# A decoder trunk on one core: the residual kept transposed, product-key scores left unscaled, sums of squares taken by matmul

## The chip, the cores and the metric

The kernel runs on one core of one Trainium2 chip. The metric is device microseconds of the whole launch; the median of three runs is compared. The traces show five engines. PE does matmuls and transposes (its weight loads are listed apart as PEld), DVE is the vector engine, ACT the scalar engine, POOL is GpSimd, and SP only issues DMAs. ACT and POOL can issue DMAs as well.

## The reference

The input x has 256 tokens (S) of 1024 features (D). Two residual layers follow, each with a mixer and a product-key expert layer ("PEER").

```python
h = x
for layer in (0, 1):
    xn = rmsnorm(h, norm_mix[layer])
    h = h + (attn_retention_mixer if layer == 0 else short_conv_mixer)(xn)
    h = h + peer(rmsnorm(h, norm_ffn[layer]))
return rmsnorm(h, final_norm)

def rmsnorm(x, g):
    return x * lax.rsqrt(mean(x * x, -1) + EPS) * g
def peer(t):                      # 8 heads, 128 x 128 experts, top 16
    q = (t @ w_q).reshape(n_tok, 8, 2, 128)
    sc = einsum('thpd,hpnd->thpn', q, sub_keys)
    s1, i1 = top_k(sc[:, :, 0], 16);  s2, i2 = top_k(sc[:, :, 1], 16)
    top_s, pos = top_k(all sums s1 + s2, 16);  eidx = the pair's expert number
    gate = softmax(top_s)
    return sum_k gate * gelu(t . u[eidx]) * v[eidx]
```

## The kernel before

**Stages.** In the profiled execution: the input projection of the even mixer to 103 us, its output projection to 128.6 us, the PEER queries of layer 0 to 183 us, the U pass over all experts to about 492 us, the V pass to 747 us, then the odd mixer, its output projection from 820.7 us, the queries from 844 us, U and V again, and the last norm from 1453 us. All four engines run orders that are written out by hand in program order, so each engine works strictly through its own list.

**Weights.** `Stream` loads weight tiles of 128 x 1024 into a ring of eight slots (SP issues, L153). Most tiles are split: ACT makes `hi` (L176), then DVE or POOL makes `lo` = raw - hi in bf16 (L178). A product takes three matmuls: hi with the high part of the activation, hi with its low part, and lo with its bf16 copy `Xb`. `u_tile` (L292) makes a 128 x 256 transposed output so. `u_pair` (L308) makes two at once, and goes through the eight feature blocks k in order, so that it can start when the first blocks of the activation `x2` are there; it calls `norm.tail(k)` between them.

**Residual.** `h` holds two halves of 128 tokens by 1024 features. The projections want activations with features on partitions. So `Norm.turn` (L435) transposes h on PE, and `Norm.parts` (L447) makes `x2[:, k, 0]` on ACT (L454), `x2[:, k, 1]` on DVE (L455) and, per two blocks, `Xb` on POOL (L458). `v_phase` (L336) makes the output projection of a mixer with tokens on partitions: for each of eight weight tiles four groups of three matmuls of 512 columns (L331 to L333), then DVE adds each quarter to h (L356). `square` (L395) sums squares on ACT.

**PEER.** Per query tile f (16 of them): a `u_tile`, four passes for scores (L1160), an ACT copy that multiplies by the norm's reciprocal root (L1163), DVE's top-16 search (L1147 to L1155) paced by a `Pump`. `Norm.rows` (L522) prepares in steps f = 2 to 5 the rows `XG` that the gathered experts meet (L535, L539, L541) and the scaled `xf` for the dense pass (L528, L532). The first 96 tokens use gathered expert rows (`Gather`, L992): 192 indirect DMAs of 128 x 1024 per layer (L1029), each eaten by one DVE instruction (L1039 for U, L1050 for V). The other 160 tokens go densely through all 128 expert tiles: L1417 in the U pass, L1520, L1560 and L1562 in the V pass, where `weight_rest` (L1435, DVE) and `weight_parts` (L1428, ACT) split the tiles.

**End of V.** The output of V is built transposed in eight PSUM banks `vo[b]`. In steps 16 to 23 PE adds h into them, by matmuls with the identity (L1550, L1551). The last three weight tiles go block by block; behind each block `fold(b)` makes `XT` (ACT L1573, DVE L1574). In layer 0 `Folded` makes `x2` from XT (L576, L577, L580), transposes XT back into h during the pair (`back`, L548; ACT L593, L609). In layer 1 `Final` squares and scales XT (L641 to L644), sums squares by matmul with a column of ones (L660), transposes (L653), and writes out.

**Start.** x comes in natural layout by one DMA on SP and one on ACT; 24 dummy matmuls (`busy`, L379) run meanwhile; `Norm.first` (L494) turns it.

Of the kernel before, what the change touches and what calls it, by code (L numbers as in the profile page):

```python
# [225 lines left out]
def trunk_kernel(ctx, tc, x, small, cst, mcst, ew_in, ew_out, ow_in, ow_out, wq, keys, pu, pe_, pv, pvn, pun, gains, out):  # L226
# [28 lines left out]
    srcs += [(ow_in[f], i > 1 and i % 2 == 1) for i, f in enumerate(OF)]  # L255
# [3 lines left out]
    h = pers.tile([P, 2, D], F32, tag="h", name="h")  # L259
# [76 lines left out]
    def v_phase(n, part, each, norm):  # L336


        accs = [acc_tile(i, nm("acc")) for i in range(4)]
        for i in range(n - 2):  # L340
            each(i)
            w = st.next()
            p = part(i)
            for a in range(4):
                run(v_mm(w, p, accs[a], a // 2, a % 2, i == 0, False))
        each(n - 2)
        each(n - 1)
        ws = [st.next(), st.next(ahead=False)]
        st.ahead(0)
        ps = [part(n - 2), part(n - 1)]  # L350
        for a in range(4):
            for j in range(2):
                run(v_mm(ws[j], ps[j], accs[a], a // 2, a % 2, False, j == 1))
                if a == 3 and j == 0:
                    norm.amid()
            v.tensor_tensor(h[:, a // 2, (a % 2) * 512:(a % 2 + 1) * 512], accs[a],  # L356
                            h[:, a // 2, (a % 2) * 512:(a % 2 + 1) * 512], OP.add)
            norm.done(a, accs[a])
# [25 lines left out]
    class Sums:  # L384
# [10 lines left out]
        def square(self, a, junk):  # L395
            th, ch = a // 2, a % 2
            act.activation(junk, h[:, th, ch * 512:(ch + 1) * 512], AF.Square, accum_out=self.w[:, th, ch:ch + 1])
# [21 lines left out]

    class Norm(Sums):  # L420
# [3 lines left out]
        def __init__(self, gi):  # L424
            super().__init__()
            self.gi = gi
            self.ps = {}

        def warm(self):

            if self.gi in (1, 3):
                nc.sync.dma_start(XG[:, 1, :], gains[self.gi // 2])
            self.table()

        def turn(self, a):  # L435


            th, ch = a // 2, a % 2
            if th == 0:
                for j in range(2):  # L440
                    self.ps[ch, j] = acc_tile(j, nm("xt")) if ch else side_tile(nm("xt"))
            for k in range(4):
                kk = ch * 4 + k
                o = (k // 2 * 2 + th) * P
                pe.transpose(self.ps[ch, k % 2][:, o:o + P], h[:, th, kk * P:(kk + 1) * P], ident)

        def parts(self, ch, ks=range(4)):  # L447

            x2 = xv["x2"]
            for k in ks:  # L450
                kk = ch * 4 + k
                ps = self.ps[ch, k % 2][:, k // 2 * S:(k // 2 + 1) * S]
                gain = G[:, (3 + self.gi) * ND + kk:(3 + self.gi) * ND + kk + 1]
                act.activation(x2[:, kk, 0, :], ps, AF.Copy, scale=gain)  # L454
                v.scalar_tensor_tensor(x2[:, kk, 1, :], ps, gain, x2[:, kk, 0, :].bitcast(F32),  # L455
                                       op0=OP.mult, op1=OP.subtract)
                if k % 2:
                    gp.tensor_copy(Xb[:, kk - 1:kk + 1, :], x2[:, kk - 1:kk + 1, 0, :].bitcast(F32))  # L458

        def done(self, a, junk):  # L460

            if a == 1:
                self.turn(0)
            if a < 3:
                self.square(a, junk)
            if a == 1:
                self.mean0(0)
                self.root(0)
            if a == 2:
                self.turn(1)  # L470
                self.rstd(0)
                self.mean0(1)
                new_x2()
            if a == 3:
                self.parts(0, (2, 3))
                self.junk = junk

        def amid(self):

            self.turn(2)  # L480
            self.parts(0, (0, 1))

        def tail(self, k):

            if k != 1:
                return
            self.turn(3)
            self.parts(1)
            self.square(3, self.junk)
            self.root(1)  # L490
            self.rstd(1)
            st.ahead(0)

        def first(self, junk):  # L494

            new_x2()
            for a in (0, 2, 1, 3):
                self.turn(a)
            self.parts(0, (0, 1))
            st._split()  # L500
            self.parts(0, (2, 3))
            st._split()
            self.parts(1)
            st._split()
            self.junk = junk

        def late(self, th):
# [5 lines left out]
            self.rstd(th)  # L513

# [7 lines left out]
        def rows(self):  # L522

            x2 = xv["x2"]

            def whole():
                XF = new_xf()
                v.tensor_tensor(XF, x2[:, :, 0, TG:].bitcast(F32), x2[:, :, 1, TG:].bitcast(F32), OP.add)  # L528

            def scaled():  # L530
                ps = self.spread()
                v.tensor_tensor(xv["xf"], xv["xf"], ps[:, None, TG:].to_broadcast([P, ND, TD]), OP.mult)  # L532

            def fetched():
                v.scalar_tensor_tensor(XG[:TG, 0, :], h[:TG, 0, :], self.scale(0)[:TG], XG[:TG, 1, :],  # L535
                                       op0=OP.mult, op1=OP.mult)
# [6 lines left out]
            return [fetched, doubled, whole, scaled]  # L543

    def back(fq, XT, th, ch):

        for b in range(4):
            pe.transpose(fq[:, b * P:(b + 1) * P], XT[:, ch * 4 + b, th * P:(th + 1) * P], ident)  # L548

    class Folded(Norm):  # L550


        def begin(self, XT, fold):

            st.parts()
            new_x2()
            self.XT = XT
            self.fq = {}
            self.fold = fold
            st.parts()  # L560

        def block(self, b, pend):

            self.fold(b)
            if b:
                self.ready(b - 1)
            if b == 5:
                st.parts()
            if b == ND - 1:
                self.ready(b)  # L570

        def ready(self, k):

            x2, XT = xv["x2"], self.XT
            gain = G[:, (3 + self.gi) * ND + k:(3 + self.gi) * ND + k + 1]
            act.activation(x2[:, k, 0, :], XT[:, k, :], AF.Copy, scale=gain)  # L576
            v.scalar_tensor_tensor(x2[:, k, 1, :], XT[:, k, :], gain, x2[:, k, 0, :].bitcast(F32),  # L577
                                   op0=OP.mult, op1=OP.subtract)
            if k % 2:
                gp.tensor_copy(Xb[:, k - 1:k + 1, :], x2[:, k - 1:k + 1, 0, :].bitcast(F32))  # L580

        def tail(self, k):

            if k == 1:
                st.parts()
# [1072 lines left out]
```

## Time and profile before

| | |
|---|---|
| median of 3 runs | 1475.15 us (1473.57 to 1475.42) |
| profiled execution, own time | 1473.25 us |
| its span, first to last instruction | 1471.5 us |
| mean granted clock of PE | 0.996 |
| PE busy | 1426.3 us, 97% of the span |
| DVE, ACT, POOL busy | 84%, 55%, 53% |
| moved by DMA | 531.78 MB, mean 361 GB/s |

The own time is 1.75 us above the span (what lies around the first and last instruction). In timeline lines the first number is the start in us, the second the time from the first to the last of the instructions merged into the line; the bracket is idle time of that engine before it and what ended it. In a table of windows the columns are the stretch, its length, busy time (and instructions) of PE, PEld, DVE, ACT and POOL, the granted clock, the mean busy share of the DMA engines, and the rate.

### The profile page before, as it was taken

Reading aid. Unit: us, or ns where it says so; the run is one execution under the profiler, and the core shown is the slowest. Engines: PE = TensorE matmul, PEld = TensorE weight load, DVE = VectorE, ACT = ScalarE, POOL = GpSimd, SP = SyncE. Lnnn points to the kernel's source line nnn. Section 1 sums busy time; section 2 is a strip of 40 time slices with the busy share of each in tenths; the row PEclk is TensorE's granted clock in tenths of the full one; section 3 lists DMA queues with packets and bytes.
Section 4 is the critical chain, followed back from the end, with each engine's and each line's share of the span. In section 5 each row is a group of like instructions: output and inputs, shape, how many; then the busy total and the mean of one; then the engine's idle time right before and its main releaser. Section 6 shows DMA issues by size and latency. Waiting matters only on the chain.

```text
span 1471.5 us, 29881 instructions
## 1 busy us (share of the span) xinstructions
PE 1426.3 (97%) x11246; PEld 1327.1 (90%) x11260; DVE 1238.5 (84%) x2505; ACT 804.0 (55%) x1872; POOL 779.3 (53%) x508
## 2 busy tenths in 40 slices
PE   9999999999999999999999999999999999999997
PEld 5667999999999999988998699999999999998887
DVE  5637999968898689989976589998788869999997
ACT  5555512248786556665563463212887746665654
POOL 6754545555655247655444374465555626665440
PEclk9999999999999999999999999999999999999999
DMA  8546899999999999999975588999999999999994
GB/s 325 191 156 247 315 370 392 400 414 411 409 406 404 400 393 412 415 416 414 411 264 181 180 303 342 403 382 406 409 412 413 410 411 392 408 415 414 415 415 181
DMA packets 113729, 531.78 MB, mean 361 GB/s; under 512 B 13168, under 2 KB 13424, under 8 KB 83888
## 3 DMA queue, kind: packets, MB, share of 16 engines
q1 hardware_dynamic: 57024, 325.06, 55.8%
q0 software_dynamic: 56416, 204.29, 35.1%
q8 instruction: 88, 1.44, 0.4%
q10 hardware_dynamic: 144, 0.52, 0.1%
q14 instruction: 57, 0.47, 0.1%
HBM read 527.93 MB, written 1.05 MB: 359 GB/s over the span
## 4 chain that ended last, share of the span: by engine, by line
PE 37%; DVE 23%; DMA 23%; issue 9%; POOL 6%; ACT 1%; DVEq 0%; SPq 0%; POOLq 0%; ACTq 0%
PE hid L1417 11%; DMA grow<-pvn,ig 9%; DMA rows<-pvn,ig 9%; PE vo L1560 5%; DMA rows<-pun,ig 4%; POOL rows L1029 4%; DVE rows L1039 4%; PE vo L1562 3%; PE hid L299 2%; PE vo L1520 2%; DVE hg L1149 2%; DVE hg L1155 2%; DVE hg L1151 2%; POOL grow L1029 2%; PE ea L331 2%
## 5 line engine op out<-in xcount | busy, mean ns | idle before, releaser
L1417 PE MATMUL hid<-xf,raw 128*128 128x160 f32 x3328 | 477.2, 301 | 7.8 <-DVE hg L1460 7.8
L1417 PEld LDWEIGHTS hid<-xf,raw 128*128 128x128 f32 x3328 | 457.8, 190 | 10.0 <-DVE hg L1460 9.9
L1428 ACT CAST vhi<-raw 128x1024 fp32r<-128x1024 f32 x222 | 229.9, 1047 | 191.7 <-DMA raw<-pv 96.7
L1029 POOL DMA_INDIRECT rows<-pvn,ig x128 | 217.7, 1700 | 183.9 <-DVE gacc L1050 150.1
L1435 DVE TENSOR_TENSOR vlo<-raw,vhi 128x1024 bf16<-128x1024 f32 x222 | 266.5, 1216 | 22.5 <-ACT vhi L1428 22.1
L1029 POOL DMA_INDIRECT rows<-pun,ig x128 | 163.4, 1277 | 116.1 <-DVE rows L1039 59.1
L1560 PE MATMUL vo<-ko,vhi 128*128 128x320 f32 x1200 | 213.6, 320 | 0.0
L178 POOL TENSOR_TENSOR lo<-raw,hi 128x1024 bf16<-128x1024 f32 x70 | 168.0, 2410 | 85.1 <-ACT hi L176 77.2
L1560 PEld LDWEIGHTS vo<-ko,vhi 128*128 128x128 f32 x1200 | 178.0, 189 | 0.0
L1562 PE MATMUL vo<-hb,vlo 128*128 128x160 bf16 x1776 | 162.0, 234 | 15.8 <-DVE vlo L1435 15.6
L1050 DVE SCALAR_TENSOR_TENSOR gacc<-rows,ghid,gacc 128x1024 f32<-128x1024 f32 x124 | 158.3, 1277 | 17.9 <-DMA rows<-pvn,ig 17.6
L1039 DVE SCALAR_TENSOR_TENSOR rows<-rows,xg 128x1024 f32<-128x1024 f32 x128 | 154.9, 1217 | 21.2 <-DMA rows<-pun,ig 20.9
L1029 POOL DMA_INDIRECT grow<-pvn,ig x64 | 117.7, 1838 | 94.7 <-DVE gacc L1050 77.2
L1457 ACT ACTIVATE hg<-hid 128x160 f32<-128x160 f32 (+14 forms) x240 | 61.9, 265 | 192.3 <-PE hid L1417 192.2
L1562 PEld LDWEIGHTS <-vlo 128*128 128x128 bf16 x1776 | 117.9, 98 | 42.4 <-DVE vlo L1435 22.2
L1029 POOL DMA_INDIRECT grow<-pun,ig x64 | 84.2, 1316 | 79.0 <-DVE grow L1039 51.9
L1367 ACT ACTIVATE ko<-ko,idxT 128x128 f16<-128x128 f16 x320 | 101.6, 391 | 38.3 <-DVE ko L1352 38.2
L176 ACT CAST hi<-raw 128x1024 fp32r<-128x1024 f32 x100 | 102.3, 1046 | 29.0 <-issue 17.4
L299 PE MATMUL hid<-x,hi 128*128 128x256 f32 x800 | 107.4, 287 | 3.9 <-DVE z L982 2.0
L299 PEld LDWEIGHTS hid<-x,hi 128*128 128x128 f32 x800 | 98.6, 190 | 5.0 <-issue 3.1
L1560 PE MATMUL vo<-xf,vhi 128*128 128x320 f32 x576 | 102.7, 321 | 0.0
L1370 ACT ACTIVATE ko<-ko,idxT 128x128 f16<-128x128 f16 x320 | 101.2, 389 | 0.0
(258 smaller groups left out, 2238.4 us busy)
## 6 DMA issues: line engine op xcount, KB each, us to landing
raw<-pv SPq DMA_DIRECT2D x128, 1024.0 KB, 9.4
raw<-pu SPq DMA_DIRECT2D x104, 1024.0 KB, 8.2
raw<-wq SPq DMA_DIRECT2D x32, 512.0 KB, 4.0
raw<-ew_in SPq DMA_DIRECT2D x28, 512.0 KB, 4.6
raw<-ow_in SPq DMA_DIRECT2D x24, 512.0 KB, 4.9
hg<-pe_ SPq DMA_DIRECT2D x22, 512.0 KB, 6.4
raw<-ew_out SPq DMA_DIRECT2D x8, 512.0 KB, 4.0
raw<-ow_out SPq DMA_DIRECT2D x8, 512.0 KB, 3.5
```

Source lines behind the costliest of these rows:

```text
L176: self.nc.scalar.copy(hi, t)
L178: eng.tensor_tensor(lo, t, hi.bitcast(F32), OP.subtract)
L299: pe.matmul(ps[:, :S], hi[:, k * P:(k + 1) * P], A2[:, k, s_, :], start=k == 0 and s_ == 0, stop=False)
L1029: gp.indirect_dma_start(self.row(s_), None, table, bass.IndirectOffsetOnAxis(IG[:, 0, s_ % STEPS:s_ % STEPS + 1].bitcast(U32), 0))
L1039: v.scalar_tensor_tensor(r, r, 1.0, XG[:, q % 2, :], op0=OP.mult, op1=OP.mult, accum_out=w)
L1050: v.scalar_tensor_tensor(self.acc[q], r, w, self.acc[q], op0=OP.mult, op1=OP.add)
L1367: act.activation(hi[:, j], lo[:, j], AF.Copy, scale=idxT[:, 1, t:t + 1])
L1417: pe.matmul(ps[:, :TD], w[k], xv["xf"][:, k, :], start=k == 0, stop=k == ND - 1)
L1428: act.copy(whi[j], raw)
L1435: v.tensor_tensor(wlo[j], raw, whi[j].bitcast(F32), OP.subtract)
L1560: pe.matmul(vo[b][:, TG:S + TD], hi[:, b * P:(b + 1) * P], hs, **m)
L1562: pe.matmul(vo[b][:, TG:S], lo[:, b * P:(b + 1) * P], hb, **m)
```

## The change

- `h` becomes 128 features by 8 blocks by 256 tokens. x comes transposed from HBM by two ACT DMAs; a natural copy `xn` goes into XG and serves for the first norm's squares alone. SP issues the weights first. 34 dummy matmuls instead of 24. `late` runs one step later.
- `v_phase` puts out transposed blocks: per weight tile and block two matmuls of 256 columns with hi and one with lo. The last two tiles go block by block. `Norm` replaces `Folded`: behind each block DVE folds into h, ACT makes the high part and a square, DVE the low part of the block before.
- All `turn` and `back` transposes and the identity matmuls of V go. `fold(b)` at the end of V is two DVE additions into h.
- Sums of squares: DVE adds the squares down to 128 x 512 during the pair, and `sums` makes four matmuls with a column of ones behind the third query tile. In the odd mixer a fourth tile is multiplied before the norm's factor is spread.
- Scores are copied unscaled; the exponential of the gates takes the factor.
- `rows` runs in f = 3 to 5: `fetched_rows` transposes 96 tokens of h with eight PE transposes; `dense` scales in eight DVE instructions instead of two.
- The last norm: squares in XG, the scaling of blocks moves from DVE to ACT, one DVE instruction fewer at the end, two of the four output DMAs go by ACT.
- The lo parts of the fourth odd input tile move from POOL to DVE.

```diff
-    h = pers.tile([P, 2, D], F32, tag="h", name="h")
+    h = pers.tile([P, ND, S], F32, tag="h", name="h")
@@ v_phase
+        for i in range(n - 2):
+            ...
+            for b in range(ND):
+                high(b, w, p, i == 0 and b < 4)
+            for b in range(ND):
+                low(b, w, p, False)
+        ws = [st.next(ahead=False) for _ in range(2)]
+        norm.begin(lambda b: v.tensor_tensor(h[:, b, :], out_of(b), h[:, b, :], OP.add))
+        for b in range(ND):
+            for w, p in zip(ws, ps):
+                high(b, w, p, False)
+            for j, (w, p) in enumerate(zip(ws, ps)):
+                low(b, w, p, j == 1)
+            norm.block(b, [])
@@ Norm
+        def begin(self, fold):
+            if self.mixes:
+                st.parts()
+            new_x2()
+            self.fold = fold
+            self.sq = [XG[:, 0, :], new_xf().rearrange("p k t -> p (k t)")[:, :D]]
+            if self.mixes:
+                st.parts()
+        def block(self, b, pend):
+            self.fold(b)
+            self.high(b)
+            act.activation(self.sq[b // 4][:, b % 4 * S:(b % 4 + 1) * S], h[:, b, :], AF.Square)
+            if b:
+                self.low(b - 1)
+            if b == ND - 1:
+                self.low(b)
+        def tail(self, k):
+            if k == 1:
+                st.parts()
+            if k == 2:
+                a, b = self.sq
+                v.tensor_tensor(a, a, b, OP.add)
+                v.tensor_tensor(a[:, :2 * S], a[:, :2 * S], a[:, 2 * S:], OP.add)
+            if k == 7 and self.mixes:
+                st.parts()
+                st.parts()
+        def sums(self):
+            ssq = side_tile(nm("ssq"))
+            for n in range(2):
+                for th in range(2):
+                    o = n * S + th * P
+                    pe.matmul(ssq[:, th:th + 1], self.sq[0][:, o:o + P], C[:, C_ONE:C_ONE + 1], ...)
+            ...
@@ end of V
-                if 16 <= i < 16 + ND:
-                    pe.matmul(vo[b][:, :P], h[:, 0, c], ident, **m)
-                    pe.matmul(vo[b][:, P:S], h[:, 1, c], ident, **m)
             def fold(b):
-                act.copy(XT[:, b, :], vo[b][:, :S])
-                v.tensor_tensor(XT[:, b, TG:], vo[b][:, S:S + TD], XT[:, b, TG:], OP.add)
+                v.tensor_tensor(h[:, b, :], vo[b][:, :S], h[:, b, :], OP.add)
+                v.tensor_tensor(h[:, b, TG:], vo[b][:, S:S + TD], h[:, b, TG:], OP.add)
@@ scores, queries
-                    act.activation(sc(th, f), ps[...], AF.Copy, scale=before.scale(th))
+                    act.copy(sc(th, f), ps[...])
-                if f == 1:
+                if f == 2:
+                    before.sums()
                     rows = before.rows()
-                if 1 < f < 6:
-                    rows[f - 2]()
+                if 2 < f < 6:
+                    rows[f - 3]()
@@ start
+        nc.scalar.dma_start(G, small)
+        for a in range(2):
+            nc.scalar.dma_start(h[:, a * 4:(a + 1) * 4, :], x[:, a * 4:(a + 1) * 4, :])
         ...
+        for th in range(2):
+            nc.scalar.dma_start(XG[:, th, :], xn[th])
+        nc.sync.dma_start(C, cst)
+        busy(34)
```

More of the change, by code (lines that the diff above doesn't have):

```diff
@@ L225, in trunk_kernel @@
 @with_exitstack
-def trunk_kernel(ctx, tc, x, small, cst, mcst, ew_in, ew_out, ow_in, ow_out, wq, keys, pu, pe_, pv, pvn, pun, gains, out):
+def trunk_kernel(ctx, tc, x, xn, small, cst, mcst, ew_in, ew_out, ow_in, ow_out, wq, keys, pu, pe_, pv, pvn, pun, gains, out):
     nc = tc.nc
@@ L339, in v_phase, with out_of, high, low @@
         accs = [acc_tile(i, nm("acc")) for i in range(4)]
+        def out_of(b):
+            return accs[b % 4][:, b // 4 * S:(b // 4 + 1) * S]
+        def high(b, w, p, first):
+            c = slice(b * P, (b + 1) * P)
+            m = dict(stop=False, skip_group_check=True)
+            pe.matmul(out_of(b), w[0][:, c], p[0], start=first, **m)
+            pe.matmul(out_of(b), w[0][:, c], p[1], start=False, **m)
+        def low(b, w, p, last):
+            pe.matmul(out_of(b), w[1][:, b * P:(b + 1) * P], p[2], start=False, stop=last, skip_group_check=True)
         for i in range(n - 2):
@@ L426, in __init__ @@
             self.gi = gi
-            self.ps = {}
+            self.mixes = gi % 2 == 0
         def warm(self):
-            if self.gi in (1, 3):
+            if not self.mixes:
                 nc.sync.dma_start(XG[:, 1, :], gains[self.gi // 2])
             self.table()
[L435 to L445, printed above, removed]
@@ L460, in done @@
[L460 to L481, printed above, removed]
@@ L483, in tail, with gain, high, low @@
[L483 to L492, printed above, removed]
+        def gain(self, k):
+            return G[:, (3 + self.gi) * ND + k:(3 + self.gi) * ND + k + 1]
+        def high(self, k):
+            act.activation(xv["x2"][:, k, 0, :], h[:, k, :], AF.Copy, scale=self.gain(k))
+        def low(self, k):
+            x2 = xv["x2"]
+            v.scalar_tensor_tensor(x2[:, k, 1, :], h[:, k, :], self.gain(k), x2[:, k, 0, :].bitcast(F32),
+                                   op0=OP.mult, op1=OP.subtract)
+            if k % 2:
+                gp.tensor_copy(Xb[:, k - 1:k + 1, :], x2[:, k - 1:k + 1, 0, :].bitcast(F32))
@@ L494, in first @@
         def first(self, junk):
             new_x2()
[L497 to L504, printed above, removed]
-            self.junk = junk
+            self.junk = junk
+            for k in range(0, ND, 2):
+                for j in (k, k + 1):
+                    self.high(j)
+                for j in (k, k + 1):
+                    self.low(j)
+                if k < 6:
+                    st._split()
@@ L957, in odd_mixer @@
                     third = u_tile(xv["x2"], Xb, side_tile(nm("hid")), ahead=False)
+                    before.sums()
+                    fourth = u_tile(xv["x2"], Xb, ahead=False)
                     rb = before.spread()
@@ L1580, in peer @@
             st.loads()
-            norm.begin(XT, fold)
+            norm.begin(fold)
             pend = []
@@ L1598, in trunk_kernel @@
         norms = [Norm(0)]
-        nc.sync.dma_start(G, small)
-        nc.sync.dma_start(C[:, :P], cst[:, :P])
-        for th in range(2):
-            (nc.scalar if th else nc.sync).dma_start(h[:, th, :], x[th])
-        nc.sync.dma_start(C[:, P:], cst[:, P:])
+        nc.scalar.dma_start(G, small)
+        for a in range(2):
+            nc.scalar.dma_start(h[:, a * 4:(a + 1) * 4, :], x[:, a * 4:(a + 1) * 4, :])
         v.memset(Z, 0.0)
```

167 lines of the change are left out of this document (53 added, 114 removed).

## The prediction

> **What bounds the kernel now.** First the page's busy times, then the waits of PE, then a table of windows through one layer.
>
> ```profile
> span 1471.5 us, 29881 instructions
> PE 1426.3 (97%) x11246; PEld 1327.1 (90%) x11260; DVE 1238.5 (84%) x2505; ACT 804.0 (55%) x1872; POOL 779.3 (53%) x508
> ...
> PE vo L1562 <- DVE vlo L1435: 15.6, 20, 2.1
> PE sc L1160 <- DVE xf L532: 1.2, 2, 0.6
> ...
> 530.00:560.00 30.00, 30.00 (x263) 28.68 (x263) 27.00 (x26) 17.72 (x22) 13.45 (x9) 1.00 1.01 398
> 560.00:650.00 90.00, 89.59 (x790) 84.67 (x789) 88.31 (x85) 58.23 (x73) 62.44 (x27) 1.00 1.02 415
> 650.00:738.00 88.00, 81.85 (x696) 76.46 (x693) 80.72 (x76) 50.38 (x62) 38.89 (x20) 0.98 1.01 412
> 1230.00:1260.00 30.00, 30.00 (x267) 28.67 (x265) 26.68 (x26) 16.33 (x20) 17.05 (x8) 1.00 1.01 411
> ```
>
> PE is without a gap nearly everywhere, so a pass of PE removed or added counts in most stages. The exception is the V pass: from 560 us DMA moves 412 to 415 GB/s whatever PE does, DVE is 98% busy, and PE then loses 6 us to DVE's lo parts. The chain of waits shows why: a gather that took 9.4 us at 440 takes 21.2 at 631.
>
> ```profile
> 440.03 9.36 DMA grow<-pvn,ig
> 631.58 21.19 DMA rows<-pvn,ig
> ```
>
> So I treat 415 GB/s as the ceiling of that stage: its end is set by bytes, not by PE.
>
> **The change part by part.** Differences are summed against the profiled execution (1473.25 us own, 1.9 below the median of the runs shown) and then put on the median 1475.15.
>
> *Start.*
>
> ```profile
> 1.66 5.17 DMA h<-x
> 1.07 5.28 PE L379 MATMUL busy<-xb 128*128 128x256 bf16 x24 [1.07 <-DVE xb L1604]
> 8.69 1.04 ACT L176 CAST hi<-raw 128x1024 fp32r<-128x1024 f32 x1
> 9.78 1.20 PE L331 MATMUL ea<-hi,x 128*128 128x512 f32 x4 [0.88 <-ACT hi L176]
> ...
> L576 ACT ACTIVATE x<-xg,small 128x256 fp32r<-128x256 f32 x8 | 4.1, 511 | 0.8 <-DVE xg L1574 0.8
> ```
>
> Before, 1 MB of x has landed at 6.83; the turns, two high parts and the cast follow, and PE begins at 9.78. After, the first megabyte on the two queues is half of x and the first weight tile, so take 6.83 again; two high parts (0.51 each) and the cast (1.04) give 8.9: **-0.9**. The dummies cover until 8.5 (34 at 5.28/24 = 0.22 each, from 1.07), so -1.3 is the best end. The turns themselves (16 passes) lay under this. xn adds 1 MB ahead of the fourth tile on shared DMA engines; its cover is the 2.8 us per step that PE then works, and if that is too short I allow +1.0 as the bad end. G and C change queues at no cost: their readers come later.
>
> *Output projections and their norms, twice.*
>
> ```profile
> 106.34 0.58 PE L331 MATMUL acc<-hi,c2e 128*128 128x512 f32 x1
> 109.12 0.58 PE L331 MATMUL acc<-hi,c2e 128*128 128x512 f32 x1
> ...
> 136.17 2.15 PE L299 MATMUL hid<-x,hi 128*128 128x256 f32 x16
> 139.05 0.61 PE L1160 MATMUL sc<-ko,hg 128*128 128x128 f32 x4
> ...
> 839.32 0.58 PE L331 MATMUL acc<-hi,c2o 128*128 128x512 f32 x1
> 841.15 0.58 PE L331 MATMUL acc<-hi,c2o 128*128 128x512 f32 x1
> ...
> 124.50 0.66 PE L445 MATMUL xt<-cst,h 128*128 128x128 f32 x4 [0.26 <-DVE h L356]
> ```
>
> A weight tile took 2.78 us in 512-column matmuls; in 256-column ones it is a `u_tile`, 2.88 from the first row at 136.17 to the scores at 139.05 (24 matmuls of 0.12). Eight tiles: **+0.8** each time. Two triples with a turn between took 1.83 instead of 1.39, so four turns are 4 x 0.44: **-1.77** each time, and layer 0's wait of 0.26 goes.
>
> A new wait: the blocks use all four accumulators within 0.75 us, the old order took 2.1.
>
> ```profile
> 103.67 0.48 PE L331 MATMUL acc<-hi,c2e 128*128 128x512 f32 x1
> 104.22 1.27 ACT L879 ACTIVATE nat<-ea,nw 128x512 f32<-128x512 f32 x2
> ```
>
> ACT empties accumulators 2 and 3 only at 104.9 and 105.5. Block 2 comes four matmuls after 103.67, at 104.15, and waits 0.75; block 3 waits another 0.32: **+1.07** in layer 0 (0 if ACT gets there earlier). In the odd mixer the accumulators are free.
>
> Stage ends are now set by DVE.
>
> ```profile
> L577 DVE SCALAR_TENSOR_TENSOR x<-xg,small,x x8: 467/542/919, 741.6 to 749.4; 128x256 fp32r<-128x256 f32 x8
> ...
> L577 DVE SCALAR_TENSOR_TENSOR x<-xg,small,x 128x256 fp32r<-128x256 f32 x8 | 5.2, 655 | 0.4 <-ACT x L576 0.2
> L1574 DVE TENSOR_TENSOR xg<-vo,xg 128x160 f32<-128x160 f32 x8 | 2.5, 317 | 0.5 <-ACT xg L1573 0.2
> L971 DVE TENSOR_TENSOR u<-hid,cg 128x256 f32<-128x256 f32 x1 | 0.4, 433 | 0.0
> ...
> 742.61 0.92 DVE L577 SCALAR_TENSOR_TENSOR x<-xg,small,x 128x256 fp32r<-128x256 f32 x1
> 742.63 0.61 POOL L580 CAST xb<-x 128x512 bf16<-128x512 f32 x1 [22.30 <-ACT x L576]
> ```
>
> A fold of 256 is like L971 (0.43), a low part from SBUF like L577: 0.467 alone, 0.92 beside a POOL cast, 0.655 in the mean, which I take since the four casts stay. With 0.04 between instructions a block costs DVE 1.165 us; PE makes one in 0.72 (2 x 2.88 / 8). With E the end of the last block, DVE begins at E - 4.8 and is done eight blocks later at E + 4.5. The pair needs the last low part at E + 3.75 (seven blocks of 0.5 us, and two matmuls): with 0.1 for the handover **+0.85** each time. ACT (0.51 and a square of 0.42 per block) is quicker. At 0.467 the wait is 0, at 0.92 it is 2.95: the two ends.
>
> The Trainium skill, SBUF — State Buffer, "SBUF: two separate sides", says that GpSimd and a DVE instruction with two SBUF inputs exclude each other for a whole instruction. The pair at 742.6 agrees (+0.45 beside a cast of 0.61). By the rule each of four casts would hold DVE a full 0.61, the low part would cost 0.77 in the mean, and this sum would come out near 1480.9.
>
> *Queries, twice.* `sums` is four matmuls, eight passes.
>
> ```profile
> 1462.71 0.61 PE L660 MATMUL ssq<-cst,fin 128*128 128x1 f32 x4
> 748.69 1.04 PE L548 MATMUL fq<-cst,xg 128*128 128x128 f32 x8
> 749.48 2.15 PE L316 MATMUL hid<-x,hi 128*128 128x256 f32 x16
> ```
>
> Four passes take 0.61 with a last duration of 0.25, so 0.12 each, eight 0.96: **+0.96**, and again in the odd mixer. `fetched_rows` is eight transposes of 0.11: **+0.88**. DVE's two additions of squares (about 1.9) and the late STT wait behind f = 2 and 3, where DVE waits for scores anyway; L528 and L532 go, eight of about 0.33 come, so I take the 0.61 wait for L532 as gone: **-0.61** (0 to -0.61). Unscaled score copies, the gates' factor and the shorter root chain are ACT and DVE work under PE: 0. If DVE fell behind, scores wait for side banks; the 0.61 is that price.
>
> *End of V in layer 0, odd mixer.* Sixteen transposes go: 748.69 to 749.48, and as much at 751.5, **-1.66**. Sums **+0.96**. DVE per block: 0.43 + 0.317 + 0.655 + 0.12 = 1.52, from 740.65 (the two lo parts of weights end there, as before):
>
> ```profile
> 738.24 2.46 DVE L178 TENSOR_TENSOR lo<-raw,hi 128x1024 bf16<-128x1024 f32 x2
> 746.68 2.18 PE L316 MATMUL hid<-x,hi 128*128 128x256 f32 x16
> ```
>
> Eight blocks end at 752.85; the pair starts at 746.68 as now, and would pass its hi part at 750.68; it passes at 753.2: **+2.5** (1.0 with low parts of 0.467, 4.65 with 0.92). The third tile's parts, the squares and the root chain then end some 2 us ahead of their readers. The fourth lo part, moved to DVE, falls behind that. The order of splits moves in the odd mixer, where PE now loses 3.9 us to DVE; I leave that, with 2 us either way.
>
> *V pass.*
>
> ```profile
> 520.70 1.42 PE L1560 MATMUL vo<-ko,vhi 128*128 128x320 f32 x8
> ...
> 524.30 0.43 PE L1550 MATMUL vo<-cst,h 128*128 128x128 f32 x2
> 526.53 0.43 PE L1550 MATMUL vo<-cst,h 128*128 128x128 f32 x2
> ```
>
> Two plain steps take 3.60, one with identity matmuls 2.23: 0.43 more, eight of them 3.4 us per layer, a saving of 0 to 3.4. What DMA can make up after 524 is the gap from 398 to 415 GB/s over 30 us, 1.2 us; in layer 1 from 411, 0.3, and a little after. I take **-1.2** and **-0.5**; late next is the lo part behind a gather.
>
> The Trainium skill, DMA: Bandwidth & Descriptors, "Where 436 GB/s comes from", puts the ceiling of 16 engines at 435 GB/s. With that room the whole 6.9 us could be had, and the time would be 1472.8; the rows do not bear it out (21 us per gather at 415).
>
> *Last norm.*
>
> ```profile
> 1462.28 0.37 ACT L1573 COPY xg<-vo 128x256 f32<-128x256 f32 x1
> 1464.16 0.16 DVE L670 TENSOR_SCALAR nw<-ssq 128x2 f32<-128x2 f32 x1 [0.76 <-PE ssq L660]
> ```
>
> From 1462.28 DVE now has a fold (0.43 + 0.317) and an addition of squares (0.43) with gaps of 0.12, to 1463.6; then come four passes (0.48), two transposes (0.22), four passes (0.48) and 0.13 of their drain. L670's successor starts at 1464.9 instead of 1464.16; one small DVE instruction less: **+0.7** (0 to 1). Output issues: two queues against a scalar instruction behind an issue, 0.
>
> **Sum.** -0.9 + 2 x (0.8 - 1.77 + 0.85) - 0.26 + 1.07 + 2 x (0.96 + 0.88 - 0.61) + (0.96 - 1.66 + 2.5) - 1.7 + 0.7 = +2.9, so **1478.0 us**, just inside the 0.2% (2.95 us) that a measurement of this kernel can tell.
>
> **The rivals.** *V pays in full*: 6.9 instead of 1.7, 5.2 less, 1472.8 us. For it: both passes lose PE time only late (the row of 560 to 650 shows 0.4 us lost, that of 650 to 738 shows 6). Against it: DMA at 415 and DVE at 98%. *DVE rules the stage ends* (the slower side): each low part meets a cast and costs 0.92; the three pairs wait 2.95, 2.95 and 4.65, 6.4 more, 1484.4 us. It decides from about 1.06 us of DVE per block on. For it: blocks now come in a row, with a cast per two. Against it: the mean of eight L577 was 0.655 beside just such casts. The lock of the Trainium skill's SBUF page would carry the time part of the way here, to 1480.9; its chance is within these 0.22. *Low parts meet no cast*: 0.467 throughout, waits of 0, 0 and 1.0, 3.2 less, 1474.8 us; the change then does what its PE count says, and little is left of either sign.
>
> **How the numbers follow.** Forecast 0.42, V in full 0.20, DVE rules 0.22, no casts 0.16. The forecast's own spread (start, odd mixer) is 2.5 either way and lies half beyond the bound, 0.20 slower; the slower rival adds 0.18, mixtures 0.01. Faster needs V in full together with a good start or no casts: 0.20. Within: 0.41. The range reaches into both outer cases, 1470.5 to 1484.5.
>
> **What would show it.** First L331 near 8.9; a wait of PE on ACT at L879's successor of about 1; PE waiting for DVE's low parts in all three pairs; waits of the V pass on lo parts grown from 15.6 toward 20; eight `sums` passes near 0.96. Wrong if those V waits do not grow (then faster), or if the pairs wait 3 us and more (then slower).

## The result and the profile after

The changed kernel is slower: 1484.1 us (median of 8 runs, 1480.63 to 1486.65) against 1474.41 for the kernel before on the same chip, ratio 1.0053 with a 95% interval of 1.0037 to 1.0069. A second set of runs gave 1487.63 against 1474.88, ratio 1.0084 (1.0069 to 1.0099). So the change costs 0.4 to 1.0%. The forecast was 1478.0, in a range that ends at 1484.5. One execution of experiment 1 below ran at a granted clock of 0.751 and took 1775.34 us; its ratio leaves that one out.

The page after, and the table of PE's waits (who waited for whom: us in total, times, longest):

```profile
span 1482.8 us, 30126 instructions
PE 1422.2 (96%) x11365; PEld 1337.8 (90%) x11374; DVE 1255.0 (85%) x2520; ACT 793.8 (54%) x1857; POOL 759.1 (51%) x507
```

```profile
PE vo L1516 <- DVE vlo L1397: 17.3, 24, 2.0
...
PE hid L299 <- DVE cg L930: 4.0, 2, 2.5
PE ea L331 <- ACT hi L176: 3.0, 1, 3.0
...
PE rtr L735 <- DVE rt L724: 2.6, 1, 2.6
PE hid L299 <- DVE z L943: 2.3, 1, 2.3
PE sc L1121 <- DVE xf L558: 2.2, 2, 1.1
PE hid L299 <- ACT hi L176: 1.5, 1, 1.5
PE hid L299 <- DVE u L932: 1.1, 1, 1.1
...
PE hid L316 <- DVE x L471: 0.7, 2, 0.4
```

PE's busy time fell by 4.1 us, yet the span grew by 11.3. The waits of L299 (the `u_tile` products; 3.9 us before) and of L735 (the transposes behind rope, that is behind the rotation of queries and keys by position) are the large ones for which the forecast has no term. Cut at the first PE instruction of each stage, the two profiled executions differ so (us; "forecast" is the sum on record, its terms put into these stages):

| stage | before | after | difference | forecast |
|---|---|---|---|---|
| up to the first product | 9.78 | 10.02 | +0.23 | -0.9 |
| even input projection | 93.88 | 97.62 | **+3.73** | 0 |
| output projection and queries, layer 0 | 79.25 | 81.45 | +2.20 | +1.92 |
| U, layer 0 | 308.68 | 308.62 | -0.06 | 0 |
| V, layer 0 | 246.78 | 245.42 | -1.35 | -1.2 |
| V's last tiles by blocks | 8.30 | 8.30 | 0 | 0 |
| odd mixer | 74.03 | 80.86 | **+6.83** | +1.8 |
| output projection and queries, layer 1 | 77.87 | 77.91 | +0.04 | +1.11 |
| U, layer 1 | 306.49 | 307.03 | +0.54 | 0 |
| V, layer 1 | 247.72 | 246.53 | -1.19 | -0.5 |
| end | 18.70 | 19.06 | +0.36 | +0.7 |
| together | | | +11.3 | +2.9 |

Two stages hold 10.6 of the 11.3 us. The forecast missed these two by 8.8 us, and the whole by 8.4.

One profile of each kernel shows the stages that PE bounds well, and the U and V passes badly. In a second profile of the changed kernel (experiment 5) both output projections with their queries have the same length to 0.01 us, but U of layer 1 took 311.68 us instead of 307.03 and V of layer 1 248.07 instead of 246.53. A difference of one or two us in a U or V pass is therefore not a result.

**The even input.** The timeline of the kernel before, where rope (its first instruction is L759) begins at 24.56 and PE's transposes need not wait:

```profile
24.56 0.88 DVE L759 SCALAR_TENSOR_TENSOR rt<-ea,nw,mcst 128x256 f32<-128x256 f32 x2
27.11 0.60 PE L776 MATMUL rtr<-cst,rt 128*128 128x128 f32 x4
```

and of the kernel after:

```profile
18.82 7.26 POOL L178 TENSOR_TENSOR lo<-raw,hi 128x1024 bf16<-128x1024 f32 x3
21.51 2.24 DVE L432 SCALAR_TENSOR_TENSOR nw<-nw 128x1 f32<-128x1 f32 x1
23.97 2.13 DVE L434 TENSOR_TENSOR nw<-nw 128x1 f32<-128x1 f32 x1
26.78 0.22 DVE L432 SCALAR_TENSOR_TENSOR nw<-nw 128x1 f32<-128x1 f32 x1
27.30 0.88 DVE L718 SCALAR_TENSOR_TENSOR rt<-ea,nw,mcst 128x256 f32<-128x256 f32 x2
29.75 1.11 PE L735 MATMUL rtr<-cst,rt 128*128 128x128 f32 x4 [2.60 <-DVE rt L724]
```

The norm's factor (L432, L434) is ready later because `late` runs a step later; rope (L718) follows it in DVE's list and starts at 27.30, and PE waits 2.60 us. A stretch of halved clock from 29.3 to 32.7 follows, which takes another 1.7 us of clock.

**The odd mixer.** The timeline after, around its first three waits:

```profile
770.87 0.37 ACT L677 CAST c2o<-z 128x256 fp32r<-128x256 f32 x1 [3.51 <-DVE z L944]
771.13 2.94 ACT L176 CAST hi<-raw 128x1024 fp32r<-128x1024 f32 x3
771.61 0.41 DVE L930 TENSOR_TENSOR cg<-hid,rs 128x256 f32<-128x256 f32 x1
772.17 2.14 PE L299 MATMUL hid<-x,hi 128*128 128x256 f32 x16 [1.53 <-ACT hi L176]
773.17 2.63 DVE L178 TENSOR_TENSOR lo<-raw,hi 128x1024 bf16<-128x1024 f32 x1 [1.14 <-ACT hi L176]
775.72 0.42 DVE L932 TENSOR_TENSOR u<-hid,cg 128x256 f32<-128x256 f32 x1
776.29 2.14 PE L299 MATMUL hid<-x,hi 128*128 128x256 f32 x16 [1.09 <-DVE u L932]
780.09 1.23 DVE L178 TENSOR_TENSOR lo<-raw,hi 128x1024 bf16<-128x1024 f32 x1 [0.52 <-ACT hi L176]
781.23 0.42 DVE L930 TENSOR_TENSOR cg<-hid,rs 128x256 f32<-128x256 f32 x1
781.80 2.15 PE L299 MATMUL hid<-x,hi 128*128 128x256 f32 x16 [2.48 <-DVE cg L930]
```

Two lists hold PE up. ACT casts c2o, which needs DVE's z, ahead of the hi part that PE needs next (771.13). DVE makes a lo part of a later weight tile ahead of the eviction that frees PE's bank (an eviction is the instruction that reads a finished product out of its PSUM bank): 2.63 us ahead of L932, and 1.23 ahead of L930.

### The profile page after: what moved, and what is told of

It reads as the page before. It is cut to its first block, busy times and chain, and to the rows that moved or that the text cites. A ratio compares the mean times of both kernels' runs of the same rounds, so it can differ in the third digit from the quotient of the medians.

```text
span 1482.8 us, 30126 instructions
## 1 busy us (share of the span) xinstructions
PE 1422.2 (96%) x11365; PEld 1337.8 (90%) x11374; DVE 1255.0 (85%) x2520; ACT 793.8 (54%) x1857; POOL 759.1 (51%) x507
## 4 chain that ended last, share of the span: by engine, by line
PE 33%; DVE 29%; DMA 22%; issue 8%; POOL 4%; ACT 3%; ACTq 0%; DVEq 0%; POOLq 0%
PE hid L1379 10%; DMA grow<-pvn,ig 8%; PE vo L1514 6%; DMA rows<-pvn,ig 6%; DMA rows<-pun,ig 4%; DVE rows L1000 4%; PE vo L1516 3%; POOL rows L990 3%; DVE grow L1000 2%; PE vo L1480 2%; PE hid L299 2%; DMA raw<-pv 2%; DVE hg L1110 2%; DVE hg L1116 2%; DVE hg L1112 2%
## 5 line engine op out<-in xcount | busy, mean ns | idle before, releaser
L990 POOL DMA_INDIRECT rows<-pvn,ig x128 | 213.0, 1664 | 194.5 <-DVE gacc L1011 151.4
L1516 PE MATMUL vo<-hb,vlo 128*128 128x160 bf16 x1776 | 162.0, 234 | 17.7 <-DVE vlo L1397 17.3
L990 POOL DMA_INDIRECT grow<-pvn,ig x64 | 110.8, 1732 | 96.4 <-DVE gacc L1011 81.2
L990 POOL DMA_INDIRECT grow<-pun,ig x64 | 81.0, 1266 | 80.3 <-DVE grow L1000 49.2
L299 PE MATMUL hid<-x,hi 128*128 128x256 f32 x800 | 108.2, 288 | 8.8 <-DVE cg L930 4.0
L299 PEld LDWEIGHTS hid<-x,hi 128*128 128x128 f32 x800 | 99.3, 191 | 10.3 <-ACT hi L176 4.5
```

What stands on the lines that cost most here:

```text
L299: pe.matmul(ps[:, :S], hi[:, k * P:(k + 1) * P], A2[:, k, s_, :], start=k == 0 and s_ == 0, stop=False)
L990: gp.indirect_dma_start(self.row(s_), None, table, bass.IndirectOffsetOnAxis(IG[:, 0, s_ % STEPS:s_ % STEPS + 1].bitcast(U32), 0))
L1516: pe.matmul(vo[b][:, TG:S], lo[:, b * P:(b + 1) * P], hb, **m)
```

## The experiments

Each was timed against the kernel before on its own chip; "ratio" means that, with its 95% interval.

**1. `late` in steps 0 and 1 again.**

```diff
-            at(1, lambda: before.late(0))
-            at(2, lambda: before.late(1))
+            at(0, lambda: before.late(0))
+            at(1, lambda: before.late(1))
```

> The changed kernel with one thing put back: the first norm's `late` runs in steps 0 and 1 again. Theory A (the shifted `late` delays the norm's factor, so rope on DVE is late and PE waits 2.60 us at L735, after which the granted clock dips): the wait at L735 goes, the even input projection takes 2.6 to 3.7 us less, the whole about 1480.5 against 1484.1 (ratio to the changed kernel 0.9975). Rival B (the natural copy of x crowds the DMA queues at the start, the weight tiles are late): the wait only moves to the hi casts, the stage keeps its 3.7 us, ratio 1.000. Third outcome C: ACT or DVE now stands waiting for that natural copy ahead of work that PE needs, and the stage grows, by up to 3 us.

Measured: 1486.13 us, ratio 1.0067 (1.0043 to 1.0092). The wait at L735 is gone and the even input takes 94.81 instead of 97.62, as theory A says. The total shows nothing of it: in the profiled execution the U pass of layer 0 took 311.41 instead of 308.62.

**2. No fourth tile ahead of the spread.**

```diff
-                    fourth = u_tile(xv["x2"], Xb, ahead=False)
-                    ps = u_tile(xv["x2"], Xb) if k > 1 else fourth
+                    ps = u_tile(xv["x2"], Xb)
```

> The changed kernel without the fourth tile ahead of the spread: the norm's factor is spread right behind the sums, as the tile order was before. Theory A (with the fourth tile ahead, every eviction of the odd mixer comes one tile later, and ACT, in strict order, holds a cast that waits for DVE ahead of the hi casts that PE needs): the PE waits of 1.5, 1.1 and 2.5 us in the odd mixer go, a wait of PE for the norm's root of about 1.3 us comes, the stage takes 3.5 to 4.5 us less, the whole about 1480 (ratio 0.9972). Rival B (the fourth tile's lo part, moved from POOL to DVE, delays DVE and so PE): the waits stay, and the wait for the root comes on top: +1 us, ratio 1.001.

Measured: 1483.49 us, ratio 1.0058 (1.0035 to 1.0080). In the odd mixer the waits of 1.5 and 1.1 us are gone, and one of 1.4 us for the norm's root has come; the wait of 2.5 us has stayed. The stage takes 77.67 instead of 80.86, but 1.7 of these 3.2 us are a stretch of halved clock that this execution did not meet. So the fourth tile explains two of the waits, not all three, and the total of a run can't resolve the difference.

**3. Both.**

> Both of the edits above: `late` in steps 0 and 1, and no fourth tile ahead of the spread. If the two causes are separate the gains add: 6 to 8 us, about 1476.5 to 1478 (ratio to the changed kernel 0.995), still 2 to 4 us above the kernel before, which the extra passes of the queries (2.0 and 1.2 us) would account for. If they share a cause, it is no better than the better of the two.

Measured: 1480.38 us (12 runs), ratio 1.0026 (1.0009 to 1.0044), below either edit alone on the same chip (1.0067 and 1.0058), with intervals that just overlap. That agrees with two separate causes. Whether the gains add in full is not shown: the changed kernel was not timed on this chip, and came out at 1.0053 and 1.0084 on two others.

**4. The kernel before without the identity matmuls of V** (so it leaves the residual out).

```diff
-                if 16 <= i < 16 + ND:
-                    ...
-                    pe.matmul(vo[b][:, :P], h[:, 0, c], ident, **m)
-                    pe.matmul(vo[b][:, P:S], h[:, 1, c], ident, **m)
```

> The kernel before without the sixteen identity matmuls in steps 16 to 23 of each V pass (the residual is then left out of the output of V). Theory A (V is bound by the bytes it moves, so PE passes taken away are worth little): 1.2 us in layer 0 and 0.5 in layer 1, together -1.7, about 1472.7 against 1474.4 (ratio to the kernel before 0.9988). Rival B (PE bounds both passes): all of 2 x 3.4 us is gained, about 1467.6 (ratio 0.9954).

Measured: 1473.33 us, ratio 0.9977 (0.9962 to 0.9992), that is 1.2 to 5.6 us less; the full 6.9 lies outside. In the profile the V passes are 1.57 and 1.15 us shorter, as they are in the changed kernel (1.35 and 1.19). Taken over all profiles of this document, though, V of layer 0 took 246.78 and 246.47 us with the identity matmuls and 244.46 to 247.05 (mean 245.9) in the twelve without; in layer 1 it took 247.72 and 246.72 with them and 246.52 to 248.86 without. So some 0.7 us of the 3.4 is gained in layer 0, and in layer 1 nothing that can be told from chance. The windows and the waits of this run show where the rest went:

```profile
560.00:650.00 90.00, 87.11 (x761) 81.72 (x760) 85.93 (x82) 56.66 (x71) 49.22 (x25) 1.00 1.02 415
```

```profile
PE vo L1556 <- DVE vlo L1435: 18.9, 31, 2.3
```

DMA moves 415 GB/s as before, PE is busy 2.5 us less in these 90 us, and its waits for lo parts grew from 15.6 to 18.9.

**5. The changed kernel again, as a base.**

> The changed kernel once more, as the base for the other runs of this call on the same chip. Theory A (the odd mixer and the even input projection lose time to waits that the order of the instructions fixes): the same PE waits as in its first profile, 2.6 us at L735, 1.5, 1.1, 2.5, 2.3 and 1.5 in the odd mixer, and a stage of 79 us there plus 1.7 for every stretch of halved clock. Rival: these waits were chance, and they lie elsewhere now. Ratio to the kernel before 1.004 to 1.007.

Measured: 1487.63 us, ratio 1.0084 (1.0069 to 1.0099). The five waits of the odd mixer are the same to 0.02 us. That at L735 is 1.34 this time: PE itself arrived later, after a stretch of halved clock from 9.9 to 13.3 us.

**6. The fourth tile's lo part back on POOL** (`i > 1` for `i > 4`).

> The changed kernel with the lo parts of the fourth odd input tile back on POOL (i > 1 in place of i > 4). Theory A (the fourth tile ahead of the spread causes the odd mixer's waits): the waits of 1.5 and 1.1 us stay, the 2.5 us wait for cg becomes at most 1.2 us shorter; the stage takes 0 to 1 us less, ratio to the changed kernel 0.9993 to 1. Rival B (DVE is late because of that lo part): DVE is 1.2 us earlier throughout, the three waits shrink by 1.2 each, 3 us less, ratio 0.998.

Measured: 1487.72 us, ratio 1.0094 (1.0078 to 1.0111). The waits are 1.52, 1.08 and 2.47 us as before, and 0.58 has come ahead of `sums`. Rival B is out; of the up to 1.2 us that theory A allowed off the third wait, none came.

**7. `late` early, a second time.**

> The kernel with `late` in steps 0 and 1 a second time, on the same chip as the changed kernel. In its first profile the even input projection was 2.8 us shorter, but the U pass of layer 0 was 2.8 us longer and began V at 497.6, where the changed kernel's V began at 497.7. Theory A (that loss was chance, by gathers that landed late): the U pass takes 308.6 again, V begins near 494.8, and the time is 2.5 to 3 us below the changed kernel (ratio 0.998). Rival B (the U pass ends by something that the start of the pass does not move, DMA or DVE): V begins at 497 to 498 again, and the time is that of the changed kernel.

Measured: 1483.84 us, ratio 1.0067 (1.0049 to 1.0085), against 1.0084 for the changed kernel beside it: 2.5 us less, with intervals that overlap. The even input took 94.82 again. V began at 496.2, between the two expectations. The U pass of layer 0 took 307.2 to 309.4 in the four profiles of kernels that keep the late `late` and 309.5 to 311.7 in the seven with the early one (the later versions below counted). Why a U pass that starts earlier should run longer was not settled; the spread between executions is as large as this difference.

**8. The three losses repaired together.** Beside both edits above: DVE adds the squares ahead of the third tile's lo part and `sums` runs behind the pair; the spread of the dense rows goes to an accumulator bank; the first half of x goes by SP.

```diff
-            nc.scalar.dma_start(h[:, a * 4:(a + 1) * 4, :], x[:, a * 4:(a + 1) * 4, :])
+            (nc.scalar if a else nc.sync).dma_start(h[:, a * 4:(a + 1) * 4, :], x[:, a * 4:(a + 1) * 4, :])
@@ odd mixer
-                    third = u_tile(xv["x2"], Xb, side_tile(nm("hid")), ahead=False)
                     before.sums()
+                    st.parts()
+                    st.parts()
+                    third = u_tile(xv["x2"], Xb, side_tile(nm("hid")), ahead=False)
@@ dense
-                ps = self.spread()
+                ps = self.spread(acc_tile(2, nm("rb")))
```

> The changed kernel without its three losses: `late` in steps 0 and 1, no fourth tile ahead of the spread; and three more edits: in the odd mixer DVE adds the squares ahead of the third tile's lo part and `sums` runs right behind the pair, so that the root's chain lies under the third tile; the dense rows' factor is spread into an accumulator bank and not into a side bank that scores wait for; the first half of x goes by SP ahead of the weights. Against the kernel with the first two edits alone (1480.4, ratio to before 1.0026): the 1.4 us wait for the root goes, two waits of 1.1 us for L558 go, and PE starts 0.5 to 1.5 us earlier, together 4 to 5 us, about 1475.5 to 1476.5, ratio to the kernel before 0.9995 (0.998 to 1.001). If the U pass swallows what comes ahead of it (rival B of the run with `late` alone), only the odd mixer and layer 1 count: 2.5 us, ratio 1.001.

Measured: 1477.9 us (12 runs), ratio 1.0022 (1.0007 to 1.0036), where 0.9995 (0.998 to 1.001) was expected: a miss. The wait for the root went, and the queries fell by 1.8 us in each layer (54.55 and 53.70). PE starts at 8.33, but the even input is then 1.5 us longer than with experiment 3's edits (95.87 against 94.34): the weights come no sooner, and PE waits 0.36, 1.01 and 0.70 on the way.

**9. Evict first.** The combined version, with the next weight tile split after the eviction of the present one:

```diff
-                    ps = u_tile(xv["x2"], Xb)
+                    ps = u_tile(xv["x2"], Xb, ahead=False)
...
                 v.tensor_tensor(cg, ps[:, :S], rs[:, 1], OP.mult)
+                if k:
+                    st.ahead(0)
```

and so behind the other two evictions of each k.

> The combined version with one edit in the odd mixer: the next weight tile is split after the eviction of the present one, not ahead of its matmuls, so that a lo part on DVE no longer stands ahead of an eviction that PE waits for. Theory A (the 2.5 us wait of PE for cg and the 2.3 us wait for z are lo parts of 1.2 to 2.6 us in front of evictions in DVE's list): both fall under 1.2 us, the stage takes 2 to 2.5 us less (plus 1.7 where a stretch at half clock goes with them), ratio to the combined version 0.998. Rival B (DVE is simply full in this stage, 84% and more): the waits move elsewhere in the stage and its length stays within 0.5 us. Rival C: hi parts now come late for PE, and the stage grows.

Measured: 1472.48 us (10 runs), ratio 0.9982 (0.9970 to 0.9995). The odd mixer takes 70.51 us instead of 78.01: 7.5 less, where 2 to 4.2 were expected. The groups of PE's instructions in that stage (busy us, mean ns, idle us before them), first of the combined version, then of this one:

```profile
L299 PE MATMUL hid<-x,hi 128*128 128x256 f32 x352 | 48.1, 290 | 6.3 <-DVE cg L930 3.9 <-DVE z L943 2.3
```

```profile
L299 PE MATMUL hid<-x,hi 128*128 128x256 f32 x352 | 47.2, 287 | 1.6 <-DVE u L934 1.0 <-ACT hi L176 0.6
```

Of the 7.5 us 4.7 are these waits and 1.7 a stretch of halved clock that followed one of them.

**10. Further repairs at the start.** No natural copy of x; squares from the transposed x, a third addition on DVE, half the matmuls of `sums`, 44 dummies.

> The combined version with two more groups of edits. First the order of evictions in the odd mixer (the other run of this call has that alone). Second: no natural copy of x; the first norm's squares are made on ACT from the transposed x, added on DVE and summed on PE as in the other norms; a third addition on DVE halves the matmuls of `sums` (4 passes in place of 8); 44 dummy matmuls. Theory A (the copy's 1 MB and PE's first 3 us of idleness cost the start, and passes of `sums` count one to one): the start's waits of 0.4, 1.0 and 0.7 us and the stretch at half clock go, 0.5 of passes come, minus 1.5 us; `sums` minus 0.5 in each of three places; with 2 to 2.5 us in the odd mixer, together 5 us under the combined version (1477.9, ratio to before 1.0022), near 1473, ratio 0.9988. Rival B (DVE's additions and ACT's squares delay the factor that rope needs): the wait for L723 grows to 2 us, the start gains nothing, ratio 1.0000.

Measured: 1480.29 us, ratio 1.0034 (1.0021 to 1.0046). A miss, and rival B by far more than it said. The timeline at the start:

```profile
14.01 11.56 POOL L178 TENSOR_TENSOR lo<-raw,hi 128x1024 bf16<-128x1024 f32 x4 [0.37 <-ACT hi L176]
20.02 3.35 DVE L504 TENSOR_TENSOR xg<-xg,xf 128x1024 f32<-128x1024 f32 x1
23.41 2.71 DVE L505 TENSOR_TENSOR xg<-xg 128x512 f32<-128x512 f32 x1
26.64 1.01 PE L542 MATMUL ssq<-cst,xg 128*128 128x1 f32 x4 [8.58 <-DVE xg L506]
```

Beside POOL's lo parts DVE's additions take 3.35 and 2.71 us (medians of the four norms: 1.22 and 0.69), and PE waits 8.58 for them. The halved `sums` gave 0.44 us in each layer's queries (54.11 and 53.25), as the count of passes says.

**11. Experiment 1 with 52 dummies instead of 34.**

> The kernel with `late` in steps 0 and 1, and 52 dummy matmuls in place of 34. In both profiles of it with 34, the dummies ended 3.4 to 3.6 us ahead of the first product, and the granted clock was 0.5 for about 3 us from 10 or 11 us on. Theory A (PE's idleness halves the clock): 18 more dummies of 0.16 to 0.18 cover it, no such stretch lies in the first 20 us, and the even input projection takes 93.4 to 93.6 us in place of 94.8. Rival: the stretch at half clock comes by chance or by another cause and stays.

One run, 1483.11 us. The windows (the third figure from the end is the granted clock) of experiment 1 and of this one:

```profile
10.00:12.00 2.00, 2.00 (x7) 1.58 (x8) 2.00 (x3) 2.00 (x5) 0.86 (x1) 0.69 1.04 412
12.00:14.00 2.00, 2.00 (x6) 0.76 (x5) 2.00 (x3) 2.00 (x5) 1.39 (x1) 0.50 1.04 418
```

```profile
10.00:12.00 2.00, 2.00 (x9) 1.45 (x10) 2.00 (x3) 2.00 (x5) 0.90 (x2) 1.00 1.04 408
12.00:14.00 2.00, 1.95 (x10) 1.11 (x9) 2.00 (x3) 2.00 (x5) 1.40 (x1) 1.00 1.04 411
```

The stretch at half clock is gone. That the dummies removed it is not shown: of seven profiles with this start and 34 dummies two, those of the changed kernel and of experiment 3, have no stretch there either, after waits of 2.95 and 3.2 us. The stage gained only 0.4 us (94.44), since PE now waits 0.70 for rope.

**12. The kernel before with the eviction edit alone** (the diff of 9).

> The kernel before with the one edit that made the combined version faster: in the odd mixer the next weight tile is split after the eviction of the present one. Its waits of PE in that stage were 0.4, 2.0 and 1.5 us. Theory A (lo parts in front of evictions are a loss that the kernel before has too, and the gain of the repaired version comes from that edit and not from the change): 2 to 3.5 us less in the stage, ratio to the kernel before 0.9977 to 0.9986, as good as the repaired version's 0.9982. Rival B (in the order of before the lo parts lie between evictions without harm; the edit is worth something only after the change): within 0.5 us, ratio 0.9997 to 1.0003, and the repaired change keeps a gain of its own.

Measured: 1468.74 us (5 runs), ratio 0.9950 (0.9934 to 0.9966), the best of all. The odd mixer takes 69.24 us, and its products wait for nothing. The row before and in this run:

```profile
L299 PE MATMUL hid<-x,hi 128*128 128x256 f32 x352 | 47.2, 287 | 3.9 <-DVE z L982 2.0 <-DVE cg L969 1.9
```

```profile
L299 PE MATMUL hid<-x,hi 128*128 128x256 f32 x352 | 47.2, 287 | 0.0
```

So the kernel before had this loss too (3.9 us of waits). The repaired change, 0.9982, owes its gain to this edit: with it in both, each against the kernel before on its own chip, the interval of the one without the change lies wholly below that of the changed one. The change, as repaired here, still costs about 0.3%, some 5 us. No run isolates what these are. The granted clock points at one part: it averages 0.9942 over the ten executions of experiment 9 against 0.9960 for the kernel before beside it, and 0.9974 against 0.9958 in this experiment, some 5 us of clock in all, though a part of that lies in the last norm, where PE waits anyway.

## Why the prediction came out as it did

The median came out 6 to 10 us above the forecast: inside the range near its upper end in the first set of runs, and 3 us beyond it in the second. What the forecast left out makes up the difference: it gave the moved `late` no cost, and it left the odd mixer at "2 us either way". Where its sum agrees to 0.35 us, in layer 0's output projection and queries, in its V pass and in the last norm, that is partly luck, as the terms show:

- **`late` a step later: not costed.** The prediction weighed the natural copy's cover and gave the even input nothing. The factor that `late` makes is read by rope in DVE's own list, and PE's transposes wait for rope. Experiments 1 and 7 put the edit back: 1.4 to 2.8 us of the stage's 3.7.
- **The odd mixer: "I leave that, with 2 us either way".** It was +6.8 where the terms made +1.8, and 1.7 of it is a stretch of halved clock. The fourth tile ahead of the spread, named in the change, was not followed through ACT's and DVE's lists; experiment 2 shows that it makes two of the waits, and 9 that the order of split and eviction makes the others, of which the kernel before had 3.9 us already.
- **The start, -0.9: +0.23.** The prediction had half of x land at 6.83 and ACT follow at once. The timeline after, then two pieces of the chain of experiment 1, whose start is the same, then the timeline of the combined version:

```profile
7.74 0.34 ACTq L1561 DMA_DIRECT2D xg<-xn  x1
8.12 0.91 ACT L466 ACTIVATE x<-h,small 128x256 fp32r<-128x256 f32 x2 [4.48 <-DMA h<-x]
```

```profile
1.19 6.44 DMA h<-x
7.64 0.34 ACTq L1561
```

```profile
1.73 1.22 ACTq L1561 DMA_DIRECT2D xg<-xn  x2
5.16 0.91 ACT L466 ACTIVATE x<-h,small 128x256 fp32r<-128x256 f32 x2 [1.99 <-DMA small<-small]
```

  Two things were missed. The first half of x landed at 7.63 and not at 6.83: two weight tiles that SP had issued at 0.75 and 1.19 landed ahead of it, at 4.74 and 7.15. And ACT's fifth issue, the second half of `xn`, went out only then, at 7.64 to 7.98 (7.74 to 8.08 in the changed kernel), so the high parts behind it in ACT's list lost another 0.4 us. In the combined version one half of x goes first on SP's queue, both issues of `xn` go out at once, and ACT begins at 5.16. The dummies were mis-sized too: 34 of them were through at 7.07, not at 8.5, and PE idled 2.95 us.
- **The wait on ACT's L838, +1.07: 1.18, so right.** The bracket shows 0.57 us, but a bracket counts only the idle time before one instruction. What the delay cost is read from the starts, of the first, fifth and ninth matmul of the output projection:

```profile
107.63 0.36 PE L347 MATMUL acc<-c2e,hi 128*128 128x256 f32 x1
108.93 0.39 PE L347 MATMUL acc<-c2e,hi 128*128 128x256 f32 x1 [0.57 <-ACT nat L838]
109.84 0.28 PE L347 MATMUL acc<-c2e,hi 128*128 128x256 f32 x1
```

  The ninth starts 2.21 us behind the first; in layer 1, where the accumulators are free, it starts 1.03 behind (832.29 and 833.32).
- **The pairs' waits, 0.85, 2.5 and 0.85: 0.85, 0.85 and none.** Again by starts: from the first product with hi to the first with lo, a pair takes 4.77 us in layer 0's output projection, 4.77 in the odd mixer, and 3.92, without a wait, in layer 1. The low parts in layer 0, in the odd mixer and in layer 1 (minimum, median, maximum in ns):

```profile
L471 DVE SCALAR_TENSOR_TENSOR x<-h,small,x x8: 469/666/919, 130.0 to 136.2; 128x256 fp32r<-128x256 f32 x8
L471 DVE SCALAR_TENSOR_TENSOR x<-h,small,x x8: 474/485/919, 747.6 to 754.9; 128x256 fp32r<-128x256 f32 x8
L471 DVE SCALAR_TENSOR_TENSOR x<-h,small,x x8: 469/659/919, 851.1 to 857.2; 128x256 fp32r<-128x256 f32 x8
```

  In the output projections four of eight low parts meet a cast, and the 0.655 was right; in the odd mixer only the last does. What was mis-sized is a block: 0.92 us and not 1.165 in the output projections, 1.09 and not 1.52 in the odd mixer, where 0.42, 0.33 and 0.485 make 1.235 and the next instruction begins before the one ahead of it ends. That layer 0 waits just the 0.85 of the forecast is luck: DVE began there 1.1 us later than forecast, behind a lo part that took 2.57 us beside POOL. The kernel before took 4.99 us in this place, 0.44 of it turns, so it lost 0.63 us that the forecast did not take off. So the rival "DVE rules the stage ends", whose 1484.4 us is almost the time measured, is wrong in its mechanism (it needs waits of 2.95, 4.65 and 2.95), and the agreement of its number is chance; "low parts meet no cast" holds in the odd mixer alone.
- **Queries: wrong in one term.** The eight `sums` passes take 0.95, as forecast. The 0.61 for L532 was taken as gone. The row of scores in the queries of layer 0, before and after:

```profile
L1160 PE MATMUL sc<-ko,hg 128*128 128x128 f32 x60 | 9.3, 278 | 0.8 <-DVE xf L532 0.6 <-ACT hg L1312 0.2
```

```profile
L1121 PE MATMUL sc<-ko,hg 128*128 128x128 f32 x60 | 9.4, 279 | 1.3 <-DVE xf L558 1.1 <-ACT hg L1124 0.2
```

  The eight dense instructions hold the side bank longer than the one before did, and the wait grew to 1.1. Experiment 8 gave them another bank, and the stage became 1.8 us shorter.
- **V under a ceiling of bytes: the rival is excluded, the sizes are not shown.** DMA still moves 415 GB/s, the waits on lo parts grew from 15.6 to 17.3 us (15.4 to 15.6 in the two profiles with identity matmuls, 17.3 to 21.0 in the twelve without), and experiment 4 excludes the 6.9 us. The differences of -1.35 and -1.19 lie within what executions of one kernel differ by, so -1.2 and -0.5 are neither confirmed nor refuted one by one.

## What to carry to other kernels

When a step moves in a program whose engines keep to written orders, follow its result to the last reader on every engine: both large misses were readers of a moved step. Read the cost of a wait from the starts of the instructions around it and not from its idle time alone. Where one engine both evicts results and prepares later inputs, evict first; look for it as a long preparation just ahead of an eviction on which the bound engine waits. And test a repair on the kernel before as well, or its gain is booked to the change.

## What the runs showed of the hardware

**Waits near 2 us cost more than themselves.** In the windows of the changed kernel a wait of 2.26 us that ends at 806.65 is followed by half clock:

```profile
804.00:808.00 4.00, 1.74 (x14) 1.48 (x12) 2.59 (x5) 1.90 (x3) 0.40 (x1) 0.95 0.21 50
808.00:810.00 2.00, 2.00 (x11) 1.78 (x11) 0.86 (x2) 1.52 (x3) 1.55 (x1) 0.50 0.45 174
810.00:812.00 2.00, 2.00 (x15) 1.69 (x14) 2.00 (x2) 0.79 (x1) 1.43 (x2) 0.75 0.18 23
```

The clock lost sums to 1.7 us, that is 3.4 us at 0.5. Over all fourteen profiles between 8 and 1462 us, 46 of 84 waits of PE of 1.9 us or more had such a stretch in them or right behind, and 2 of 196 waits of 0.9 to 1.9 us; each stretch cost 1.7 us of clock, but for 5.1 at the wait of 8.58 us. The same wait meets it in one execution and not in another (2.48 us at 781.80 in the changed kernel did not, 2.47 us at 782.48 in experiment 1 did). On the mean a wait past 1.9 us thus costs up to 0.9 us more. The profile of experiment 12 shows no such stretch until 1460 us; over its five executions the granted clock averages 0.9974 against 0.9958 before, some 2.4 us, which with the 4.8 us in the odd mixer makes 7.2 of the 8.2 us it gained. The Trainium skill, TensorE: Matmul & The Clock Gate, in its part on the HAM clock gate, has the clock at half after at least one idle window of about 3.4 us, and the window runs free of the kernel. The length of the stretches and the part of chance agree with these rows; the idleness does not: 1.9 to 2.6 us were often enough.

**A tiny DVE instruction can take 2 us beside POOL.** In the timeline of the even input above, L432 and L434 write one element per partition; they take 2.24 and 2.13 us while POOL makes lo parts of 2.4, and L432 takes 0.22 when POOL is between two. The kernel before shows the same (2.05 and 2.12 us at 18.96 and 21.24). The Trainium skill, SBUF — State Buffer, "SBUF: two separate sides", says that a DVE instruction with two SBUF inputs, such as these, and a GpSimd instruction that reads SBUF exclude each other for a whole instruction. Here the trace agrees, and in experiment 10 too (3.35 for 1.22); of the odd mixer's low parts only the last met a cast at full cost.
